# MoE weights read in 8 KB and 4 KB runs, with a gather that reads h at a step of four floats

## The chip, the cores and the metric

The kernel runs on one core of one Trainium2 chip. The metric is the device time in microseconds, the median of the runs shown.

## What is computed

The program is two blocks of a model on 256 tokens of 1024 features, float32. The part that matters is the mixture of experts that ends each of the two layers of the second block: a router picks one of 4 groups and 2 of its 4 experts for each token, and each of the 16 experts is a gated network of width 512,

`y = (silu(x @ w_gate[e]) * (x @ w_up[e])) @ w_down[e]`

with w_gate and w_up of 1024 x 512 and w_down of 512 x 1024. All weights of all experts are read: 16 x 3 x 2 MB = 96 MB in each layer, 192 MB in all.

## The kernel before, in words

`MoeQueue` (lines 56 to 117) is the stream of weights for a memory attention and the MoE layer behind it. Its constructor lists the chunks in the order of use: for every pair of experts p = 0 to 7, four chunks of w_gate, four of w_up and four of w_down, each of 1 MB. `fetch` (78) issues one load for each free slot, on SP's queue (line 85); `done` (113) gives the slots of used chunks back and fetches again. Slots are tiles of 8 KB on each of 128 partitions; some slots come in two halves, and their chunk is then loaded as two pieces. A chunk of w_gate or w_up holds 512 of the 1024 input features; partition p of it holds rows p, 128 + p, 256 + p and 384 + p of the 512, four runs of 2 KB in memory. A chunk of w_down holds all 512 inner features and 512 of the 1024 output columns, again four runs of 2 KB on each partition.

`moe` (1571) makes eight passes q = 0 to 7, one for each pair of experts, with the two experts side by side in the 128 output partitions (64 slots for tokens each). The steps of a pass, by line:

- L1639: gate, then up. The gathered tokens `xg` are the stationary operand, the weights the moving one. For a gate or up: 8 features of 128 x 2 experts = 16 matmuls of 128 x 64 by 512 columns. A float32 matmul has two records in the trace, so a pass has 64 records.
- L1644, L1645: silu on ACT and the product on DVE give `hid`.
- L1625 (`scatter`): the pass before's result Y is added to the tokens' sums, 8 matmuls, in float32r.
- L1612, L1614 (`select_T`): the selection is transposed (sT), and the tokens' weights (cs) are fetched.
- L1654, L1656: `hid` is transposed to `hT`.
- L1604 (`gather`, for pass q + 1): token selection by matmul. A block of 128 tokens by 128 features of h is the stationary operand, the 0/1 selection `sel` the moving one (128 columns); 8 feature blocks x 2 token blocks = 16 matmuls, 32 records. ACT and DVE copy the result to `xg` (L1606). There are 8 gathers in each layer: one ahead of pass 0, and one in each of passes 0 to 6.
- L1668: down, 16 matmuls into two accumulators `pd[0]`, `pd[1]` of 512 columns each, 32 records: first all of half hf = 0, then hf = 1.
- L1674, L1675: ACT and DVE split each half of pd into two float32r parts, Y.

In pass 7 the code scatters half 0 before the second half of down is evicted, and a branch for overfull experts (`moe_dense`, L1665 to L1667) stands in the middle of down.

The order of the instructions on each engine is settled when the program is built: the framework takes the code's order as a priority and may put an instruction with ready inputs ahead of one that it thinks must wait. TensorE then runs its list in that fixed order.

The lines that the change touches:

Of the kernel before, what the change touches and what calls it, by code (L numbers as in the profile page):

```python
# [11 lines left out]
F32 = mybir.dt.float32  # L12
# [41 lines left out]


class MoeQueue:
    """Weight chunks of a memory attention and a MoE layer in the order of use: slots of a ring, and some filled only once."""

    def __init__(self, nc, wq, wo, wg, wu, wd):
        self.nc, self.ring, self.free, self.loaded, self.used = nc, [], [], [], 0  # L60
        self.queue = []
        if wq is not None:
            self.queue += [(wq[:, c * 256:c * 256 + 256].rearrange("(k p) f -> p k f", p=128), 8) for c in range(4)]
            self.queue += [(wo[k * 128:k * 128 + 256].rearrange("(a p) f -> p a f", p=128), 2) for k in range(0, 8, 2)]
        for p in range(8):
            for w in (wg, wu, wd):
                for c in range(2):
                    for e in (2 * p, 2 * p + 1):
                        cut = w[e, :, c * 512:c * 512 + 512] if w is wd else w[e, c * 512:c * 512 + 512, :]
                        self.queue.append((cut.rearrange("(k p) f -> p k f", p=128), 4))  # L70

    def add(self, pool, n):
        self.free += [(pool, "mw", True, 1)] * n
# [4 lines left out]
    def fetch(self, n=99):  # L78
        while n and self.free and len(self.loaded) < len(self.queue):
            ap, a = self.queue[len(self.loaded)]  # L80
            slot = self.free.pop(0)
            v, m = [], a // slot[3]
            for u in range(slot[3]):
                t = slot[0].tile([128, 2048 // slot[3]], F32, tag=slot[1], name="mw").rearrange("p (k f) -> p k f", k=m)
                self.nc.sync.dma_start(t, ap[:, u * m:u * m + m])
                v.append(t)
            self.loaded.append(v[0] if slot[3] == 1 else v)
            self.ring.append(slot)
            n -= 1
# [30 lines left out]
class Block:  # L120
# [1450 lines left out]
    def moe(self, h, x32, r, li, last=False):  # L1571
        nc, i, tc = self.nc, self.i, self.tc
        vec, act, pe = nc.vector, nc.scalar, nc.tensor
        tt, mm = vec.tensor_tensor, pe.matmul
        mq, self.moe_queue, self.pending = self.moe_queue, None, None
        C, pos, iota = r["C"], r["pos"], r["iota"]
        with ExitStack() as es:
            mo = es.enter_context(tc.tile_pool(name="mo", bufs=1))
            mb = es.enter_context(tc.tile_pool(name="mb", bufs=self.extra))
            if last:  # L1580
                mq.once(self.mp, "mk")
                mq.once(self.mp, "mv")
            mq.add(mb, self.extra)
            mq.once(self.xp, "xl")
            mq.once(self.gp, "nrm", 2)
            mq.once(self.gp, "g", 2)
            mq.once(self.xp, "xh")
            mq.fetch()

            def select(q):  # L1590
                sel = mo.tile([128, 2, 128], F32, name="sel", bufs=2)
                for t in range(2):
                    tt(sel[:, t].rearrange("p (e s) -> p e s", e=2), iota.unsqueeze(1).broadcast_to([128, 2, 64]),
                       pos[:, t, 2 * q:2 * q + 2].unsqueeze(2).broadcast_to([128, 2, 64]), op=ALU.is_equal)
                return sel

            def gather(sel):
                xg = mo.tile([128, 8, 128], F32, name="xg")
                for g in range(2):
                    p = self.ps()  # L1600
                    for u in range(4):
                        f = 4 * g + u
                        for t in range(2):
                            mm(p[:, u * 128:u * 128 + 128], h[:, t, f * 128:f * 128 + 128], sel[:, t],  # L1604
                               start=t == 0, stop=t == 1)
                    (act.copy, vec.tensor_copy)[g](xg[:, 4 * g:4 * g + 4], p.rearrange("p (u s) -> p u s", u=4))  # L1606
                return xg

            def select_T(q, sel):
                p = self.ps()  # L1610
                for t in range(2):
                    pe.transpose(p[:, t * 128:t * 128 + 128], sel[:, t], self.ident)  # L1612
                for t in range(2):
                    mm(p[:, 256:258], sel[:, t], C[:, t, 2 * q:2 * q + 2], start=t == 0, stop=t == 1)  # L1614
                sT = mo.tile([128, 256], F32R, name="sT")
                cs = mo.tile([128, 1], F32, name="cs")
                act.copy(sT, p[:, 0:256])
                for e in range(2):
                    vec.tensor_copy(cs[64 * e:64 * e + 64], p[64 * e:64 * e + 64, 256 + e:257 + e])
                return sT, cs  # L1620

            def scatter(q, hf, sT, Y):
                for t in range(2):
                    for n in range(2):
                        mm(acc[t][hf], sT[:, t * 128:t * 128 + 128], Y[hf][n], start=q == 0 and n == 0, stop=q == 7 and n == 1)  # L1625

            acc = self.accs()
            stats = [self.small(8, "ln") for _ in range(2)]
            sel = select(0)
            xg = gather(sel)  # L1630
            prev = None
            for q in range(8):
                gu = []
                for m in range(2):
                    w = mq.take(4)
                    ps = self.ps()
                    for k in range(8):
                        for e in range(2):
                            mm(ps[64 * e:64 * e + 64], xg[:, k, e * 64:e * 64 + 64], mq.slab(w[2 * (k // 4) + e], k % 4),  # L1639
                               start=k == 0, stop=k == 7)  # L1640
                    mq.done(4)
                    gu.append(ps)
                hid = mo.tile([128, 512], F32, name="hid")
                act.activation(hid, gu[0], AF.Silu)  # L1644
                tt(hid, hid, gu[1], op=ALU.mult)  # L1645
                if q == 0:
                    over = nc.values_load(r["cnti"][0:1, 0:1], min_val=0, max_val=512)
                if prev is not None:
                    for hf in range(2):
                        scatter(q - 1, hf, *prev)  # L1650
                sT, cs = select_T(q, sel)
                p = self.ps()
                for f in range(4):
                    pe.transpose(p[:, f * 128:f * 128 + 128], hid[:, f * 128:f * 128 + 128], self.ident)  # L1654
                hT = mo.tile([128, 4, 128], F32, tag="hT", name="hT")
                vec.tensor_copy(hT, p.rearrange("p (f s) -> p f s", f=4))  # L1656
                if q < 7:
                    sel = select(q + 1)
                    xg = gather(sel)
                w = mq.take(4)  # L1660
                pd = [self.ps(), self.ps()]
                for hf in range(2):
                    for k in range(4):
                        if q == 7 and hf * 4 + k == 6:
                            with tc.If(over > 64):  # L1665
                                self.moe_dense(mo, h, li, r["Co"])
                        for e in range(2):  # L1667
                            mm(pd[hf][64 * e:64 * e + 64], hT[:, k, 64 * e:64 * e + 64], mq.slab(w[2 * hf + e], k),  # L1668
                               start=k == 0, stop=k == 3)
                mq.done(4)  # L1670
                Y = []
                for hf in range(2):
                    y = [mo.tile([128, 512], F32R, tag="hT" if hf and n else "Y%d%d" % (hf, n), name="Y") for n in range(2)]
                    act.activation(y[0], pd[hf], AF.Copy, scale=cs)  # L1674
                    vec.scalar_tensor_tensor(y[1], pd[hf], cs, y[0], op0=ALU.mult, op1=ALU.subtract)  # L1675
                    Y.append(y)
                    if q == 7 and hf == 0:
                        scatter(7, 0, sT, Y)
                        self.deep_add(h, acc, stats, 0)
                prev = sT, Y  # L1680
            scatter(7, 1, *prev)
            self.deep_add(h, acc, stats, 1)
        x = None if last else self.xT()
        self.layer_norm_both(h, acc, stats, li, 2, *(x or ()))
        return x
# [323 lines left out]
```

## Time and profile before

| | |
|---|---|
| median of 3 runs | 1748.44 us (1744.04 to 1748.51) |
| span of the profiled execution, first to last instruction | 1741.2 us |
| TensorE busy | 1619.0 us, 93% of the span |
| mean granted TensorE clock | 0.958 |
| bytes moved by DMA | 375.39 MB in 230353 packets |

The span is that of one profiled execution. Only its span is given; the three timed runs are 2.8 to 7.3 us above it, which is what lies around the first and last instruction. The two MoE stages are about 1062 to 1296 us and 1497 to 1730 us after the start.

### The profile page before, as it was taken

To read this page: it belongs to the slowest core of one execution; us is meant where nothing else is said; L and a number is where in the kernel's file an instruction comes from. 1 tells how busy PE (TensorE), PEld (TensorE's weight loads), DVE (VectorE), ACT (ScalarE), POOL (GpSimd) and SP (SyncE) were. 2 spreads that over 40 slices of the span, in tenths; PEclk is the share of its full clock that TensorE was granted. 3 is DMA by queue.
4 is the path that set the end of the run, shared out by engine and by line. 5 is a ranking of instruction groups with operands and counts; after the bars stand their busy time and mean duration, and the time that the engine had idled before them with its cause. 6 is when DMAs were issued, how large, how long until landed. Compare 5 with 4: busy or idle time off the path is not lost. (4 is left out here: it accounts for less than half of the span.)

```text
span 1741.2 us, 26063 instructions
## 1 busy us (share of the span) xinstructions
PE 1619.0 (93%) x10383; PEld 1213.0 (70%) x10383; DVE 888.9 (51%) x1864; ACT 699.2 (40%) x1288; POOL 186.8 (11%) x153
## 2 busy tenths in 40 slices
PE   7899999879899999999999899999979989999995
PEld 6778999758788778999887785444427778544532
DVE  3567655498857567665568643111126964311112
ACT  5676455345434546554467432010116643201101
POOL 4610000056623110000101000000000000000000
PEclk9999999989969998999999899999989999999998
DMA  9324653432321329643661948999948177899983
GB/s 346 134 97 148 216 187 129 125 106 85 97 69 58 108 81 308 206 159 121 226 233 49 339 173 330 387 387 387 386 146 284 74 254 258 325 387 386 387 321 127
DMA packets 230353, 375.39 MB, mean 216 GB/s; under 512 B 17092, under 2 KB 105932, under 8 KB 230220
## 3 DMA queue, kind: packets, MB, share of 16 engines
q1 hardware_dynamic: 215616, 359.88, 58.7%
q10 hardware_dynamic: 14604, 13.71, 2.6%
q8 instruction: 86, 1.41, 0.3%
q14 instruction: 47, 0.39, 0.1%
HBM read 372.52 MB, written 1.05 MB: 215 GB/s over the span
## 5 line engine op out<-in xcount | busy, mean ns | idle before, releaser
L191 ACT CAST wh<-w 128x1024 fp32r<-128x1024 f32 (+1 forms) x253 | 260.3, 1039 | 232.5 <-PE mm L216 123.1
L192 DVE TENSOR_TENSOR wl<-w,wh 128x1024 fp32r<-128x1024 f32 (+1 forms) x214 | 257.1, 1210 | 151.9 <-ACT wh L191 151.4
L1639 PE MATMUL mm<-mw,xg 128*64 128x512 f32 x1024 | 230.2, 594 | 0.0
L217 PE MATMUL mm<-xh,wl 128*128 128x256 f32 x800 | 227.1, 284 | 0.0
L216 PE MATMUL mm<-xl,wh 128*128 128x256 f32 x800 | 226.9, 284 | 0.0
L215 PE MATMUL mm<-xh,wh 128*128 128x256 f32 x800 | 226.6, 283 | 0.0
L1639 PEld LDWEIGHTS mm<-mw,xg 128*64 128x64 f32 x1024 | 73.7, 137 | 144.0 <-issue 142.5
L215 PEld LDWEIGHTS mm<-xh,wh 128*128 128x128 f32 x800 | 151.9, 190 | 1.9
L216 PEld LDWEIGHTS mm<-xl,wh 128*128 128x128 f32 x800 | 151.3, 189 | 2.3 <-DVE xl L252 0.3
L217 PEld LDWEIGHTS mm<-xh,wl 128*128 128x128 f32 x800 | 151.5, 189 | 0.0
L1668 PE MATMUL mm<-mw,hT 128*64 128x512 f32 x512 | 118.7, 596 | 1.7 <-issue 1.7
L215 PE MATMUL acc<-wh,xh 128*128 128x512 f32 x284 | 112.9, 403 | 1.6 <-ACT xh L249 0.9
L216 PE MATMUL acc<-wl,xh 128*128 128x512 f32 x284 | 114.0, 402 | 0.0
L217 PE MATMUL acc<-wh,xl 128*128 128x512 f32 x284 | 113.3, 401 | 0.0
L192 POOL TENSOR_TENSOR wl<-w,wh 128x1024 fp32r<-128x1024 f32 x39 | 93.4, 2404 | 79.4 <-ACT wh L191 73.9
L1645 DVE TENSOR_TENSOR hid<-hid,mm 128x512 f32<-128x512 f32 x16 | 11.0, 687 | 168.3 <-PE mm L1639 168.3
L1668 PEld LDWEIGHTS mm<-mw,hT 128*64 128x64 f32 x512 | 36.6, 137 | 69.2 <-issue 67.5
L1675 DVE SCALAR_TENSOR_TENSOR Y<-mm,cs,Y 128x512 fp32r<-128x512 f32 x32 | 24.0, 751 | 114.2 <-ACT Y L1674 114.2
L1674 ACT ACTIVATE Y<-mm,cs 128x512 fp32r<-128x512 f32 x32 | 22.0, 687 | 146.8 <-PE mm L1668 146.8
L215 PE MATMUL acc<-wh,fh 128*128 128x512 f32 x176 | 69.5, 395 | 0.0
L217 PE MATMUL acc<-wh,fl 128*128 128x512 f32 x176 | 69.5, 396 | 0.0
L216 PE MATMUL acc<-wl,fh 128*128 128x512 f32 x176 | 69.3, 394 | 0.0
(529 smaller groups left out, 3127.8 us busy)
## 6 DMA issues: line engine op xcount, KB each, us to landing
mw<-in_moe_w_gate_dram SPq DMA_DIRECT2D x61, 1024.0 KB, 14.2
mw<-in_moe_w_up_dram SPq DMA_DIRECT2D x60, 1024.0 KB, 14.3
mw<-in_moe_w_down_dram SPq DMA_DIRECT2D x57, 1024.0 KB, 14.1
w<-in_ffn_w_gate_dram SPq DMA_DIRECT2D x22, 1024.0 KB, 5.9
w<-in_ffn_w_up_dram SPq DMA_DIRECT2D x22, 1024.0 KB, 6.7
w<-in_ffn_w_down_dram SPq DMA_DIRECT2D x22, 1024.0 KB, 6.3
w<-in_attn_w_qkv_dram SPq DMA_DIRECT2D x12, 1024.0 KB, 10.8
w<-in_a_w_in_dram SPq DMA_DIRECT2D x12, 1024.0 KB, 10.6
```

What stands on the lines that cost most here:

```text
L191: nc.scalar.copy(r[0], raw)
L192: (lo_eng or nc.vector).tensor_tensor(r[1], raw, r[0], op=ALU.subtract)
L215: mm(out, lhs[0], rhs[0], start=start, stop=False)
L216: mm(out, lhs[0], rhs[1], start=False, stop=False)
L217: mm(out, lhs[1], rhs[0], start=False, stop=stop)
L1639: mm(ps[64 * e:64 * e + 64], xg[:, k, e * 64:e * 64 + 64], mq.slab(w[2 * (k // 4) + e], k % 4), start=k == 0, stop=k == 7)
L1645: tt(hid, hid, gu[1], op=ALU.mult)
L1668: mm(pd[hf][64 * e:64 * e + 64], hT[:, k, 64 * e:64 * e + 64], mq.slab(w[2 * hf + e], k), start=k == 0, stop=k == 3)
L1674: act.activation(y[0], pd[hf], AF.Copy, scale=cs)
L1675: vec.scalar_tensor_tensor(y[1], pd[hf], cs, y[0], op0=ALU.mult, op1=ALU.subtract)
```

## The change

Three things change. The chunks of w_gate and w_up are cut so that partition p holds rows 4p to 4p + 3 of the 512, one run of 8 KB (two of 4 KB where the slot comes in halves). So that the input features fit, the gather takes as its stationary operand features 4q + u of a half instead of 128 adjacent ones: 128 elements of h at a step of four floats, 16 bytes. And for passes 0 to 6 the chunks of w_down hold 256 inner features and all 1024 output columns, two runs of 4 KB, with the loop of L1668 turned round: the inner feature block outside, the output half inside. Pass 7 keeps its w_down chunks and loop order. Numbers and sizes of loads and of matmuls stay.

```diff
@@ MoeQueue.__init__
         for p in range(8):
-            for w in (wg, wu, wd):
+            for w in (wg, wu):
                 for c in range(2):
                     for e in (2 * p, 2 * p + 1):
-                        cut = w[e, :, c * 512:c * 512 + 512] if w is wd else w[e, c * 512:c * 512 + 512, :]
-                        self.queue.append((cut.rearrange("(k p) f -> p k f", p=128), 4))
+                        self.queue.append((w[e, c * 512:c * 512 + 512, :].rearrange("(p k) f -> p (k f)", k=4), 4))
+            for c in range(2):
+                for e in (2 * p, 2 * p + 1):
+                    if p == 7:
+                        self.queue.append((wd[e, :, c * 512:c * 512 + 512].rearrange("(k p) f -> p k f", p=128), 4))
+                    else:
+                        self.queue.append((wd[e, c * 256:c * 256 + 256, :].rearrange("(k p) f -> p k f", p=128), 2))
@@ MoeQueue.fetch
-            v, m = [], a // slot[3]
+            v, m, n1 = [], a // slot[3], 2048 // slot[3]
             for u in range(slot[3]):
-                t = slot[0].tile([128, 2048 // slot[3]], F32, tag=slot[1], name="mw").rearrange("p (k f) -> p k f", k=m)
-                self.nc.sync.dma_start(t, ap[:, u * m:u * m + m])
-                v.append(t)
+                t = slot[0].tile([128, n1], F32, tag=slot[1], name="mw")
+                if len(ap.shape) == 2:
+                    self.nc.sync.dma_start(t, ap[:, u * n1:u * n1 + n1])
+                    v.append(t.rearrange("p (k f) -> p k f", k=m))
+                else:
+                    t = t.rearrange("p (k f) -> p k f", k=m)
+                    self.nc.sync.dma_start(t, ap[:, u * m:u * m + m])
+                    v.append(t)
@@ moe, gather
+            hk = h.rearrange("p t (c q k) -> p t c k q", c=2, k=4)
...
-                            mm(p[:, u * 128:u * 128 + 128], h[:, t, f * 128:f * 128 + 128], sel[:, t],
-                               start=t == 0, stop=t == 1)
+                            mm(p[:, u * 128:u * 128 + 128], hk[:, t, g, u], sel[:, t], start=t == 0, stop=t == 1)
@@ moe, down
-                for hf in range(2):
-                    for k in range(4):
-                        if q == 7 and hf * 4 + k == 6:
-                            with tc.If(over > 64):
-                                self.moe_dense(mo, h, li, r["Co"])
-                        for e in range(2):
-                            mm(pd[hf][64 * e:64 * e + 64], hT[:, k, 64 * e:64 * e + 64], mq.slab(w[2 * hf + e], k),
-                               start=k == 0, stop=k == 3)
+                order = [(hf, k) for hf in range(2) for k in range(4)] if q == 7 else [(hf, k) for k in range(4) for hf in range(2)]
+                for n, (hf, k) in enumerate(order):
+                    if q == 7 and n == 6:
+                        with tc.If(over > 64):
+                            self.moe_dense(mo, h, li, r["Co"])
+                    for e in range(2):
+                        if q == 7:
+                            b = mq.slab(w[2 * hf + e], k)
+                        else:
+                            b = mq.slab(w[2 * (k // 2) + e], k % 2)[:, hf * 512:hf * 512 + 512]
+                        mm(pd[hf][64 * e:64 * e + 64], hT[:, k, 64 * e:64 * e + 64], b, start=k == 0, stop=k == 3)
```

## Rows read from the trace of the kernel before

**Rows 1.** The page: span, busy time, and GB/s in 40 slices.

```profile
span 1741.2 us, 26063 instructions
PE 1619.0 (93%) x10383; PEld 1213.0 (70%) x10383; DVE 888.9 (51%) x1864; ACT 699.2 (40%) x1288; POOL 186.8 (11%) x153
GB/s 346 134 97 148 216 187 129 125 106 85 97 69 58 108 81 308 206 159 121 226 233 49 339 173 330 387 387 387 386 146 284 74 254 258 325 387 386 387 321 127
```

**Rows 2.** Windows of layer 0's MoE: busy by engine, PEclk, DMA share, GB/s.

```profile
1080.00:1197.00 117.00, 117.00 (x625) 55.00 (x626) 18.82 (x38) 12.48 (x22) 0.00 (x0) 1.00 1.05 387
1272.00:1284.00 12.00, 10.39 (x47) 3.67 (x44) 1.38 (x2) 0.11 (x1) 0.08 (x1) 1.00 0.02 7
```

**Rows 3.** Waits of the weight-load side, 1060 to 1280 us: total, times, longest.

```profile
PEld mm L1639 <- DMA mw<-in_moe_w_down_dram: 0.7, 2, 0.4
```

**Rows 4.** Timeline of PE, layer 0, pass 3 and the start of 4.

```profile
1142.92 13.90 PE L1639 MATMUL mm<-mw,xg 128*64 128x512 f32 x64
...
1159.79 3.74 PE L1604 MATMUL mm<-sel,h 128*128 128x128 f32 x32
1163.45 7.09 PE L1668 MATMUL mm<-mw,hT 128*64 128x512 f32 x32
1170.37 13.90 PE L1639 MATMUL mm<-mw,xg 128*64 128x512 f32 x64
```

**Rows 5.** Timeline of PE, layer 0, passes 5 and 6.

```profile
1197.80 7.89 PE L1639 MATMUL mm<-mw,xg 128*64 128x512 f32 x34
...
1229.68 1.07 PE L1639 MATMUL mm<-mw,xg 128*64 128x512 f32 x2
...
1247.41 0.66 PE L1654 MATMUL mm<-c_ident,hid 128*128 128x128 f32 x4 [0.78 <-DVE hid L1645]
...
1251.57 4.50 PE L1668 MATMUL mm<-mw,hT 128*64 128x512 f32 x18
1256.06 0.74 PE L1625 MATMUL acc<-Y,sT 128*128 128x512 f32 x2
1256.72 3.65 PE L1668 MATMUL mm<-mw,hT 128*64 128x512 f32 x14
1260.30 0.73 PE L1625 MATMUL acc<-Y,sT 128*128 128x512 f32 x2
1260.96 1.07 PE L1639 MATMUL mm<-mw,xg 128*64 128x512 f32 x2
```

**Rows 6.** Timeline of PE, layer 1, starts of passes 6 and 7.

```profile
1660.74 1.02 PE L1639 MATMUL mm<-mw,xg 128*64 128x512 f32 x2
...
1694.45 1.07 PE L1639 MATMUL mm<-mw,xg 128*64 128x512 f32 x2
```

**Rows 7.** The page: all packets; and a window while 4 KB runs of attn_w_qkv load.

```profile
DMA packets 230353, 375.39 MB, mean 216 GB/s; under 512 B 17092, under 2 KB 105932, under 8 KB 230220
10.00:16.00 6.00, 5.77 (x26) 4.40 (x25) 5.37 (x8) 5.10 (x8) 0.55 (x1) 1.00 1.04 397
```

**Rows 8.** Groups by shape, PEld: busy, mean ns of one.

```profile
L1639 PEld LDWEIGHTS mm<-mw,xg 128*64 128x64 f32 x1024 | 73.7, 137 | 144.0 <-issue 142.5 <-DMA mw<-in_moe_w_down_dram 0.7 <-SPq L1665 0.3
...
L1614 PEld LDWEIGHTS mm<-C,sel 128*128 128x128 f32 x64 | 8.4, 191 | 0.0
```

**Rows 9.** Timeline of PEld, pass 3 of layer 0.

```profile
1158.85 0.53 PEld L1614 LDWEIGHTS mm<-C,sel 128*128 128x128 f32 x4
```

**Rows 10.** Groups by shape, DVE: L829 reads at a 64 B step, the others contiguously.

```profile
L829 DVE TENSOR_TENSOR tmp<-aT 128x225 f32<-128x225 f32 x2 | 1.1, 546 | 0.0
L829 DVE TENSOR_TENSOR tmp<-aT 128x100 f32<-128x100 f32 x2 | 0.6, 313 | 0.0
L1885 DVE TENSOR_TENSOR s<-acc,sc 128x384 f32<-128x384 f32 x8 | 4.4, 552 | 0.2
L544 DVE TENSOR_TENSOR ft<-gt,mm 128x256 f32<-128x256 f32 x44 | 18.3, 416 | 7.4 <-PE mm L217 5.0 <-ACT gt L542 2.4
```

**Rows 11.** The page: eviction of Y on ACT.

```profile
L1674 ACT ACTIVATE Y<-mm,cs 128x512 fp32r<-128x512 f32 x32 | 22.0, 687 | 146.8 <-PE mm L1668 146.8
```

## The prediction

> **What bounds the kernel now.** I read the page first: TensorE is busy 93% of the span, and the DMA slices show where the MoE weights pass: four slices in a row at 386 or 387 GB/s in layer 0, and the like in layer 1 [rows 1]. So two candidates for the bound of these stages, and the stage's own views must say which. The windows of layer 0's MoE show both full: in 117 us TensorE has no idle time, its granted clock is 1.00 (the higher level, 2.4 GHz), and the transfer engines have a share of 1.05 at 387 GB/s [rows 2]. The waits decide: in 220 us the largest wait of the gate and up matmuls for loads is 0.7 us, in two places together [rows 3]. TensorE sets the pace; the loads had a head start and just keep it. They are done early too: after 1272 us the window holds 7 GB/s [rows 2], and TensorE has been in the last pass since 1260.96 [rows 5].
>
> The timeline then gives the price list of a pass: pass 3 of layer 0 takes 1170.37 - 1142.92 = 27.45 us, its gather 1163.45 - 1159.79 = 3.66 us, its down 1170.37 - 1163.45 = 6.92 us, all without a gap [rows 4]. Passes 5 and 6 are longer with the same matmuls: their scatters stand inside down and between the first gate matmuls, and `hid` is waited for [rows 5]. That is an order fixed at the build, not a wait for data.
>
> **The transfers.** 64 chunks of gate and up in a layer go from 512 runs each to 128, and 28 of the 32 down chunks from 512 to 256: 64 x 384 + 28 x 256 = 31,744 packets fewer in a layer, 63 thousand in both, of 230 thousand [rows 7]. What a longer run does to the rate: 2 KB runs have 387 GB/s [rows 2], a window in which 4 KB runs make most of the bytes has 397 [rows 7], 2.6% more; no row has 8 KB. The 96 MB of a layer (100.7 MB in the profile's units, 260 us at 387) would be through 7 us sooner. I cost this at nothing: TensorE's work hides it, and a faster stream could return little more in this stage than those 0.7 us; if the rate fell by the same 2.6%, the end 7 us later would still come with TensorE busy in the last pass. Ends: -1 to +1 us. SP issues as many loads as before, so nothing moves in its queue.
>
> **The gather.** This is the term that decides. Each layer has 8 gathers of 32 records, 16 x 32 = 512 records in all, every one on TensorE's path. A record now costs 3.66 / 32 = 114 ns [rows 4]. What sets this? A load of 128 columns has a duration of 191 ns, one of 64 columns 137 [rows 8], so 54 / 64 = 0.84 ns a column and 108 ns for 128. Where the matmul behind the load has only two columns, four loads take 0.53 us, so they follow each other by (0.53 - 0.19) / 3 = 113 ns [rows 8, 9]. So loads at full pace take 113 of the 114 ns: there is a slack of 1 ns, and whatever the step of 16 bytes adds to a load shows at once. It can't shorten a record, as the load was contiguous and its matmul stays. The lower end is 0.
>
> No row shows TensorE reading at a step. The nearest is VectorE at L829, which reads one operand at a step of 64 bytes: from 100 to 225 elements it goes from 313 to 546 ns, 1.86 ns an element, against (552 - 416) / 128 = 1.06 in contiguous operations [rows 10]. A step costs VectorE 0.80 ns an element, a factor of 1.75. Carried to the load in three ways: by the factor, 108 x 0.75 - 1 = 80 ns a record, 41 us; by the added time, 128 x 0.80 - 1 = 101 ns, 52 us; by 1.86 ns an element outright, 128 x 1.86 + 5 - 114 = 129 ns, 66 us. Between 0 and 66 I take the added time, 52 us: the memory is the same one, and L829 is the only row of a stepped read that I can put a slope to. A gather would take 6.9 us, and the pass 30.7.
>
> **Down.** Loop order and cut: same 32 records, same four chunks taken at once. `pd[0]` is now complete two records before the end instead of at half time. In passes 0 to 4 its eviction (ACT 0.69 us [rows 11], DVE after it) has the 13.9 us of the next gate and up [rows 4] before scatter needs Y, so it costs nothing. Where a scatter stood inside down (three places: passes 5 and 6 of layer 0, pass 6 of layer 1) it can't stand there any more. Such a down took 1260.30 - 1251.57 less 0.66 for the two scatter matmuls, 8.07 us against 6.92 [rows 4, 5]: 1.15 us three times, 3.5 us back at best. If the scatter then stands right behind down, it waits for the eviction, 0.69 us three times, 2.1 us. I take -1; ends -3.5 and +2.
>
> **Sum.** 52 - 1 = +51 us. The profile's span would go from 1741.2 to 1792; the median lies 7.2 us above that span, so 1748.4 + 51 = 1799. Own range of this case: from 41 - 4.5 to 66 + 3, that is 1785 to 1817.
>
> **Rival 1: the step is free, and the order stays.** TensorE may have enough reads under way that a load takes 108 ns at any step. For it: a load's 0.84 ns a column is already twice the 0.42 ns in which the array takes a moving column at 2.4 GHz, so something else than the memory may set it. Against: L829. Then only down and the transfers remain: 1747, between 1744 and 1751, which a measurement can't tell from no change (0.3% is 5.2 us). The Trainium skill, "SBUF — State Buffer", section "Door 1: The DMA port swizzle (why `[64,N]` ≈ `[32,N]`)", says that consecutive reads must hit a 16-byte line twice for full bandwidth, and then that "how far you can stride for free depends on dtype: 4 fp32"; the step here is exactly four floats. By that last sentence the time would be the 1747 of this rival; by the first one the load pays; no run so far shows which.
>
> **Rival 2: faster, because the order of passes 5 to 7 is settled anew.** The build put scatters early in passes 5 and 6. Were the new program ordered like pass 3 throughout, layer 0 would get back: from the start of pass 5 to that of pass 7 63.16 us [rows 5], less two passes of 27.45 and 1.3 us for four scatter matmuls of pass 6 already done, 7.0 us. In layer 1 pass 6 takes 1694.45 - 1660.74 = 33.71 [rows 6], less 27.45 and 1.3, 5.0 us. Together 12 us: 1736, if the step is free. It decides for faster from about half of that on. For it: loads in longer runs may count as earlier at the build, and the scatter's old place inside down is closed. Against: in both layers the loads would still be the slower of the two (12.6 MB a pass at 387 GB/s is 32.5 us against 27.45), so that the build has the same reason to put other work first. With the step's cost it gives 1787, inside the range of the first case.
>
> **Rival 3: the transfers gain more than I think**, 8 KB runs being well above 397 GB/s. It changes nothing while TensorE sets the pace, so it is hidden anyway, and ends at 1747 too.
>
> **How the numbers follow.** The stepped load costs something over 0.3% with a chance of 0.50; free with about the same order 0.26 (rivals 1 and 3); free with a better order 0.24. The predicted time is that of the first, 1799. The cases lie on both sides: the range reaches from 1737, which leaves out the better half of rival 2, to 1815, which leaves out the dearest loads. Faster 0.24, same 0.26, slower 0.50.
>
> **What would show it.** In the profile after: PEld at the gather's line, records 200 ns or more apart and a gather near 6.9 us in the timeline (3.66 if rival 1 holds); pass 3 at 30.7 us; packets near 167 thousand; GB/s in the MoE slices between 387 and 397, or less where TensorE takes the weights more slowly; waits of L1639 for loads still under 2 us in a layer; passes 5 and 6 with down in one piece, and 27 to 28 us (less the gather's surplus) if rival 2 is right. I am wrong if the gather keeps 3.7 us, or if TensorE turns out to wait for loads.

## The result, and the profile after

| | before | after |
|---|---|---|
| median, measured side by side, 4 runs each | 1748.47 us (1744.04 to 1752.74) | 1804.86 us (1800.51 to 1807.12) |
| ratio after / before | | 1.0331, 95% interval 1.0304 to 1.0358 |
| span of the profiled execution | 1741.2 us | 1805.3 us |

The change makes the kernel 3.3% slower, 56 us. Each time lies about 1.8 us above the span of its own execution (1807.12 and 1805.3 for the profiled one after, the slowest of its four). So the 2.8 to 7.3 us between the times before and the one span given there, and the 7.2 us that the prediction names, are for the most part differences between executions, and not what lies around the first and last instruction.

The page of the kernel after, its lines for the span, TensorE (PE) and its weight loads (PEld), VectorE (DVE) and ScalarE (ACT), the transfer rate in 40 slices and the packets:

```profile
span 1805.3 us, 26048 instructions
PE 1682.7 (93%) x10383; PEld 1279.4 (71%) x10383; DVE 886.3 (49%) x1864; ACT 699.3 (39%) x1288; POOL 186.9 (10%) x153
GB/s 345 136 77 178 188 195 94 173 49 114 98 48 83 85 198 226 205 184 98 302 70 252 219 244 392 396 408 378 114 125 253 44 351 269 331 408 393 171 329 92
DMA packets 167761, 375.39 MB, mean 208 GB/s; under 512 B 17092, under 2 KB 105932, under 8 KB 152140
```

PE has 63.7 us more busy time and PEld 66.4 more, for the same number of instructions [rows 1]. The packets fell by 62,592. So the loads got the longer runs that were wanted, and TensorE got slower. Where, the groups by shape tell (busy time, mean ns of one; idle before). First the gather's weight load in the kernel before, then load and matmul in the kernel after:

```profile
L1604 PEld LDWEIGHTS mm<-sel,h 128*128 128x128 f32 x512 | 60.2, 196 | 0.7 <-PE mm L1522 0.7
```

```profile
L1617 PE MATMUL mm<-sel,h 128*128 128x128 f32 x512 | 122.7, 400 | 0.6 <-DVE lg L1543 0.6
L1617 PEld LDWEIGHTS mm<-sel,h 128*128 128x128 f32 x512 | 120.8, 329 | 0.7 <-PE mm L1532 0.7
```

A load of 128 columns takes 133 ns longer, 1.04 ns a column. The timeline of PE in pass 3 of layer 0 (start, length, engine, line, count), after:

```profile
1132.71 13.90 PE L1651 MATMUL mm<-mw,xg 128*64 128x512 f32 x64
...
1149.55 7.63 PE L1617 MATMUL mm<-sel,h 128*128 128x128 f32 x32
1157.10 7.09 PE L1684 MATMUL mm<-mw,hT 128*64 128x512 f32 x32
1164.02 13.90 PE L1651 MATMUL mm<-mw,xg 128*64 128x512 f32 x64
```

Gate and up last 13.90 us and down 1164.02 - 1157.10 = 6.92 us, both as before [rows 4]. The gather alone has grown, from 3.66 to 1157.10 - 1149.55 = 7.55 us, that is from 114 to 236 ns a record, and the pass from 27.45 to 31.31 us. 512 records by 122 ns are 62.5 us.

From the first gather to the last scatter, layer 0's MoE grew from 1295.40 - 1055.59 = 239.8 to 1331.40 - 1061.63 = 269.8 us and layer 1's from 1728.46 - 1489.46 = 239.0 to 1792.63 - 1525.17 = 267.5: 58.5 us together. The other 5.6 us of the difference of the two spans lie outside the two MoE stages, where nothing was changed; the medians, 56.4 us apart, don't have them.

The windows of layer 0's MoE after (us, busy time of PE, PEld, DVE, ACT, POOL, then PEclk, DMA share, GB/s), and the one row of waits of the gate and up loads for a transfer, 1060 to 1335 us:

```profile
1090.00:1220.00 130.00, 130.00 (x606) 71.95 (x607) 17.55 (x37) 12.30 (x21) 0.00 (x0) 1.00 0.99 398
1226.00:1300.00 74.00, 72.33 (x317) 36.57 (x314) 9.73 (x18) 7.23 (x12) 0.00 (x0) 1.00 0.63 250
```

```profile
PEld mm L1651 <- DMA mw<-in_moe_w_down_dram: 0.6, 2, 0.3
```

TensorE is busy without a gap in the first of these windows and for 72.33 of 74 us in the second, at a granted clock of 1.00 (the higher level), and waits 0.6 us in all for weights, against 0.7 before [rows 3] and 0.3 more on a load of w_gate. It hardly waits less, since there was nothing to wait less for. Passes 5 and 6 keep their early scatter, but down stands now in one piece, with the scatter behind it:

```profile
1226.65 7.89 PE L1651 MATMUL mm<-mw,xg 128*64 128x512 f32 x34
...
1252.99 7.14 PE L1684 MATMUL mm<-mw,hT 128*64 128x512 f32 x32
1260.10 1.52 PE L1637 MATMUL acc<-Y,sT 128*128 128x512 f32 x4
1261.55 1.07 PE L1651 MATMUL mm<-mw,xg 128*64 128x512 f32 x2
...
1295.87 1.07 PE L1651 MATMUL mm<-mw,xg 128*64 128x512 f32 x2
```

### The profile page after: what moved, and what is told of

Its sections match the earlier page's. It is cut to its first block, busy times and chain, and to the rows that moved or that the text cites. A ratio compares the mean times of both kernels' runs of the same rounds, so it can differ in the third digit from the quotient of the medians.

```text
span 1805.3 us, 26048 instructions
## 1 busy us (share of the span) xinstructions
PE 1682.7 (93%) x10383; PEld 1279.4 (71%) x10383; DVE 886.3 (49%) x1864; ACT 699.3 (39%) x1288; POOL 186.9 (10%) x153
## 3 DMA queue, kind: packets, MB, share of 16 engines
q1 hardware_dynamic: 153024, 359.88, 54.5%
q8 instruction: 86, 1.41, 0.3%
## 5 line engine op out<-in xcount | busy, mean ns | idle before, releaser
L1617 PE MATMUL mm<-sel,h 128*128 128x128 f32 x512 | 122.7, 400 | 0.6 <-DVE lg L1543 0.6
L1617 PEld LDWEIGHTS mm<-sel,h 128*128 128x128 f32 x512 | 120.8, 329 | 0.7 <-PE mm L1532 0.7
```

Source lines behind the costliest of these rows:

```text
L1617: mm(p[:, u * 128:u * 128 + 128], hk[:, t, g, u], sel[:, t], start=t == 0, stop=t == 1)
```

## The experiments

The theory: the whole loss is the stepped weight load, and longer runs give nothing because TensorE sets the pace. Rivals: something else of the change costs (the loop of down, the transfers, the order), or the step costs less than it seems and an order covers part of it.

### Take the parts apart

**adjacent**: the kernel after, gathering adjacent columns of h again.

```diff
-mm(p[:, u * 128:u * 128 + 128], hk[:, t, g, u], sel[:, t], ...)
+mm(p[:, u * 128:u * 128 + 128], h[:, t, f * 128:f * 128 + 128], sel[:, t], ...)
```

> The changed kernel with the gather reading 128 adjacent features again, and nothing else undone, so that it multiplies the wrong features by the weights and its output is not the reference's. Theory S (the stepped weight load is the whole loss): a gather is back from 7.56 to 3.67 us, 16 gathers give back 62 us, and the time is 1740 to 1748. Rival T (the longer runs or the down loop cost something too): some of the loss stays, 1755 or more; if they were the whole of it, 1800 to 1805.

Measured: 1747.24 us (1741.16 to 1751.91), ratio to before 1.0012 (0.9998 to 1.0026). The loss is gone, and no gain is to be seen, although the transfers run faster than in any kernel with 2 KB runs. The page's rates:

```profile
GB/s 346 132 98 146 218 175 140 112 118 74 108 67 56 109 76 313 199 163 122 219 239 48 339 172 330 414 416 416 351 86 287 73 277 233 325 415 417 335 311 124
```

416 instead of 387 GB/s in the MoE's full slices [rows 1], 7.5% more, is worth nothing that can be measured here.

**step4**: the kernel before, with the step of the gather alone.

```diff
+hk = h.rearrange("p t (c q k) -> p t c k q", c=2, k=4)
-mm(p[:, u * 128:u * 128 + 128], h[:, t, f * 128:f * 128 + 128], sel[:, t], ...)
+mm(p[:, u * 128:u * 128 + 128], hk[:, t, f // 4, f % 4], sel[:, t], ...)
```

> The kernel before with only the gather's step of four floats, weights and loops as they were, so that the features don't fit the weights and the output is not the reference's. Theory S: 512 records at 236 instead of 114 ns, +62 us, 1806 to 1813, slightly above the changed kernel, which has the down loop's gain of up to 3.5 us. Rival T: 1748 to 1760.

Measured: 1804.76 us (1802.01 to 1806.31), ratio 1.0346 (1.033 to 1.0362), and to the nanosecond the loads of the kernel after:

```profile
L1606 PEld LDWEIGHTS mm<-sel,h 128*128 128x128 f32 x512 | 120.8, 329 | 0.7 <-PE mm L1522 0.7
```

One edit in one operand, with the old transfers, the old down and the old order, makes the whole loss.

**down_only**: the kernel before, with the change's cut of w_down and its loop.

```diff
-            for w in (wg, wu, wd):
+            for w in (wg, wu):
...
+                        self.queue.append((wd[e, c * 256:c * 256 + 256, :].rearrange("(k p) f -> p k f", p=128), 2))
...
-                for hf in range(2):
-                    for k in range(4):
+                order = [(hf, k) for hf in range(2) for k in range(4)] if q == 7 else [(hf, k) for k in range(4) for hf in range(2)]
```

> The kernel before with only the w_down part: 4 KB runs and the turned loop in passes 0 to 6; gate, up and gather as before. Theory S: within 4 us of the kernel before, 1744 to 1750, since the transfers are hidden and a down that scatters no longer cut is worth at most 1.2 us in three places. Rival T: clearly slower, by over 5 us.

Measured: 1744.49 us (1741.52 to 1747.97) against 1744.44 before, ratio 0.9997 (0.9984 to 1.001). Neither the order of the loop nor 4 KB runs (389 to 397 GB/s in the full slices of its page) move the time.

### What the step costs, by its size

**step2** and **step8**: as step4, with `k=2` and `k=8` in the rearrangement, so that neighbours in the load are 8 or 32 bytes apart.

> The kernel before with the gather at a step of two floats (8 bytes), weights as they were, so that the output is not the reference's. If the price is paid for each new 16 bytes that a load touches (1.88 ns each, hidden as far as the load has four or two elements from it), two elements share one: 128 x 0.94 + 5 = 125 ns a record, +6 us, 1751 to 1757. If it is paid for each element that isn't adjacent to the one before: as with four floats, 1806 to 1813. If a step of two is free: 1744 to 1750.

> The kernel before, with only the gather's stationary operand read at a step of 8 floats (32 bytes); the features of h reach the gate and up matmuls in another order than that of their weights, so the output is another. If the price is that of opening a 16-byte stretch for every element, a step of 4 floats has reached its end: PEld mean 329 ns, gather 7.5 us a pass, time 1800 to 1810 us. If the price grows with the distance (as it grew from a step of 2, +6 ns a record, to a step of 4, +122 ns), it goes on: PEld over 450 ns, gather over 11 us, time over 1860 us.

Measured: step2 1749.96 us (1749.53 to 1751.76), ratio 1.0034 (1.0021 to 1.0047); step8 1806.32 us in one run, so without an interval. The loads, of step2 and then of step8:

```profile
L1606 PEld LDWEIGHTS mm<-sel,h 128*128 128x128 f32 x512 | 66.6, 209 | 0.7 <-PE mm L1522 0.7
```

```profile
L1606 PEld LDWEIGHTS mm<-sel,h 128*128 128x128 f32 x512 | 123.3, 334 | 0.7 <-PE mm L1522 0.7
```

With gather and down of step2's timeline, then of step8's:

```profile
1138.11 3.93 PE L1606 MATMUL mm<-sel,h 128*128 128x128 f32 x32
1141.97 7.09 PE L1669 MATMUL mm<-mw,hT 128*64 128x512 f32 x32
```

```profile
1144.06 7.77 PE L1606 MATMUL mm<-sel,h 128*128 128x128 f32 x32
1151.77 7.09 PE L1669 MATMUL mm<-mw,hT 128*64 128x512 f32 x32
```

A gather at a step of two floats takes 1141.97 - 1138.11 = 3.86 us, 121 ns a record, 6 or 7 more than adjacent columns. At four floats a record costs 122 more than adjacent columns, and eight floats add little to that: (1151.77 - 1144.06) / 32 = 241 ns against 236. So from 16 to 32 bytes the price doesn't grow with the distance. It is there at both steps, where no two neighbours lie within the same 16 bytes, and all but gone at 8 bytes, where two do. No step between 8 and 16 bytes was run.

**moving4**: the kernel before, with the weights of gate and up, the moving operand, read at a step of four floats.

```diff
-mm(ps[...], xg[...], mq.slab(w[2 * (k // 4) + e], k % 4), ...)
+mm(ps[...], xg[...], mq.slab(w[2 * (k // 4) + e], k % 4).rearrange("p (n s) -> p s n", s=4), ...)
```

> The kernel before, with the moving operand of the gate and up matmuls (the weights, 512 columns) read at a step of 4 floats and the gather as it was; the output's columns come in another order. It asks whether the price belongs to the stationary load alone. If every read of the array at a 16-byte step pays as the weight load does (1.04 ns a column more), a record of 512 columns lasts some 530 ns longer, and 256 pairs of records give 136 us if a pair runs side by side, 272 us if not: 1880 to 2020 us. If the moving side streams a step of 16 bytes at its own pace, the matmul stays at 594 ns and the time at 1742 to 1750 us.

Measured: 1988.61 us in one run, 243.7 us more than the 1744.95 before. Its group, and gate and up of one pass in its timeline:

```profile
L1639 PE MATMUL mm<-mw,xg 128*64 128x512 f32 x1024 | 476.7, 1079 | 0.0
```

```profile
1144.65 28.97 PE L1639 MATMUL mm<-mw,xg 128*64 128x512 f32 x64
```

Gate and up of a pass take 28.97 instead of 13.90 us [rows 4]; 16 passes by 15.07 us are 241 us, nearly the whole difference. 32 pairs of records share the 15.07 us: 471 ns for 512 columns, 0.92 ns a column. The moving side pays as the stationary one does. (The expectation counted 256 pairs of records where the two layers have 512, each pair running side by side, so its lower figure belongs with the doubled count, at 272 us; 244 were measured.)

### Can the runs be had without the price?

**copy**: the kernel after, but h is copied once a layer into the order of the runs, and the gather loads adjacent columns of the copy. The copy takes the memory of one spare slot of the weight queue.

```diff
-hk = h.rearrange("p t (c q k) -> p t c k q", c=2, k=4)
+hv = h.rearrange("p t (c q k) -> p t c k q", c=2, k=4)
+hc = mo.tile([128, 2, 1024], F32, name="hc")
+hk = hc.rearrange("p t (c k q) -> p t c k q", c=2, k=4)
+for t in range(2):
+    for c in range(2):
+        (act.copy, vec.tensor_copy)[c](hk[:, t, c], hv[:, t, c])
-b.extra = 2
+b.extra = 1
```

> The changed kernel with the 8 KB runs and the cut of w_down kept, but the strided read moved out of TensorE: once a layer four copies of 128x512 (two on ScalarE, two on VectorE) write h in the order of the runs, and all 512 gather records load adjacent columns of that copy. If the loss is the price of the stepped weight load, paid 512 times and here only in four copies of about 1.1 us, it is gone: PEld 196 to 203 ns, gather 3.7 us, and 1744 + (0 to 2 x 2.2) = 1744 to 1752 us. If something else of the change costs (the one slot of memory fewer for the queue of weights, the order of features, the loop of the down projection), a part of the 56 us stays: over 1760 us.

Measured: 1749.76 us (1748.27 to 1751.72), ratio 1.0023 (1.0008 to 1.0037). The full slices of its page run at 414 to 418 GB/s, and some 52 of the 56 us are back. The copies themselves, from the view of that tile (count, then least, median and greatest ns, first and last start):

```profile
L1612 ACT COPY hc<-h x4: 1138/1142/1150, 1046.1 to 1489.2; 128x512 f32<-128x512 f32 x4
L1612 DVE COPY hc<-h x4: 611/630/642, 1046.7 to 1489.9; 128x512 f32<-128x512 f32 x4
```

So the change can be had almost for nothing, and is worth nothing: the step was paid 512 times by TensorE, and is paid here by two engines that have time. What TensorE sees of the copies is a later start of the router's matmuls in each layer, the row of layer 0 before and then with the copies:

```profile
1047.51 1.92 PE L1519 MATMUL mm<-x,wr 128*20 128x128 f32 x16 [0.29 <-ACT x L258]
```

```profile
1047.79 1.92 PE L1529 MATMUL mm<-x,wr 128*20 128x128 f32 x16 [0.88 <-ACT x L268]
```

That is 0.59 us more, and the same in layer 1, 1.2 of the 4 us. The rest can't be put down to the copies: in this profile the 28 last records of the two first gathers take 5.79 and 5.55 us at granted clocks of 0.54 and 0.57, against 3.32 and 4.95 us at 1.00 and 0.65 before; but in the profile of `order` below, which has no copy, they take 6.02 and 5.63 us at 0.52 and 0.56.

### The order of passes 5 to 7

**order**: the kernel before, with the scatter held back until the last up matmul is issued.

```diff
-mm(ps[64 * e:64 * e + 64], xg[...], ...)
+up = mm(ps[64 * e:64 * e + 64], xg[...], ...)
 ...
-for hf in range(2):
-    scatter(q - 1, hf, *prev)
+with tc.issue_after(up.ins):
+    for hf in range(2):
+        scatter(q - 1, hf, *prev)
```

> The kernel before, with one edit: the scatter of the pass before is held back until the last up matmul is issued, in all passes, so that passes 5 and 6 of both layers run in the order of pass 3. Rival 2's premise, that the early scatter costs 3 us in each of these four passes, gives 1744 - 12 = 1733 us (1731 to 1738) and pass lengths of 27.5 us throughout. If the early scatter only moves a wait (PE waits then for the evictions elsewhere in the same pass), the time stays 1742 to 1748 us, and passes 5 and 6 still last about 30 us though the scatter stands in its place.

Measured: 1737.06 us (1732.77 to 1740.09), ratio 0.9948 (0.9929 to 0.9966), faster by 8 us in the medians and 9 by the ratio. The timeline of PE in pass 6 of layer 0:

```profile
1232.05 7.89 PE L1639 MATMUL mm<-mw,xg 128*64 128x512 f32 x34
1239.87 0.44 PE L1612 MATMUL mm<-c_ident,sel 128*128 128x128 f32 x2
...
1240.58 7.08 PE L1639 MATMUL mm<-mw,xg 128*64 128x512 f32 x30
1247.59 2.14 PE L1625 MATMUL acc<-Y,sT 128*128 128x512 f32 x8
1249.57 0.60 PE L1655 MATMUL mm<-c_ident,hid 128*128 128x128 f32 x4
...
1253.67 7.09 PE L1669 MATMUL mm<-mw,hT 128*64 128x512 f32 x32
1260.59 7.89 PE L1639 MATMUL mm<-mw,xg 128*64 128x512 f32 x34
```

The scatter has its place, `hid` isn't waited for, and a pass takes 1260.59 - 1232.05 = 28.54 us instead of 31.28 [rows 5]. It isn't the 27.45 of pass 3: the transposes of the selection still cut gate and up in two, and 7.89 + 7.08 is 1.07 us more than the 13.90 of the uncut piece. From the gather of pass 0 (the one for pass 1) to the last scatter, layer 0 goes from 217.9 to 212.3 us and layer 1 from 215.5 to 211.9: 9.2 us, in line with the times.

**order_again**, **down_order** (with the w_down of down_only) and **copy_order** (the copy kernel with the scatter held back), measured together:

> The kernel with the scatter held back in every pass, once more, as the measure for the two runs beside it: 0.995 of the kernel before (0.993 to 0.997), 1733 to 1740 us.

> The scatter held back, and w_down loaded in runs of 4 KB with its loop as in the change; gate and up and the gather as before. If transfers stay hidden, the two edits add up to the gain of the order alone, since the w_down part gave nothing by itself: 1733 to 1740 us, within 3 us of the run with the order alone. If the order has brought PE up to the transfers (its profile has one wait of PE on a w_up load, 0.9 us), the faster loads of w_down show now: 1 to 3 us under it.

> The changed kernel with the copy of h (long runs everywhere, gather from adjacent columns) and the scatter held back. Additive: +4 for the copies and -8 for the order make 1740 us (1736 to 1745), over the run with the order alone. If the transfers bind once the order is mended, the rate of 8 KB runs takes back the copies' price: 1736 us or under, no slower than the order alone.

| | median (range), us | ratio to before (1744.14 us) |
|---|---|---|
| order_again | 1734.94 (1729.86 to 1738.74) | 0.9941 (0.9922 to 0.996) |
| down_order | 1733.39 (1731.73 to 1735.3) | 0.994 (0.9923 to 0.9958) |
| copy_order | 1735.54 (1734.06 to 1737.8) | 0.9952 (0.9934 to 0.9969) |

All three beat both kernels, and their intervals overlap: the order makes the gain, and the longer runs add nothing to it that can be told. The copies' 4 us aren't seen again in copy_order. That the long runs take them back there, as its second hypothesis has it, finds no support in the profiles: TensorE's loads wait for weights for 0.6 us in the two MoE stages of order_again together and for 0.9 in those of copy_order, so there are no 4 us of waiting to win back. The copies may cost less than the first comparison said, but the intervals are as wide as the difference, and this stays open.

## Why the prediction was right, and where its sizes were off

**What bounds the stage: right.** TensorE, with transfers that just keep up. `adjacent` shows it: rates up by 7.5%, time within 0.3%.

**The gather: right in its mechanism, too small by a sixth.** The prediction saw that a load at full pace leaves 1 ns of slack in a record, so that whatever the step adds shows at once; `step4` and the timeline after confirm it. The term that was mis-sized is the price of the step: I took VectorE's added time, 0.80 ns an element, 101 ns a record and 52 us. Measured are 122 ns a record. TensorE's load adds 1.04 ns a column to its 0.84, 1.88 together, which is close to VectorE's 1.86 ns an element outright [rows 10]; this third way, 129 ns and 66 us, was the nearest of the three. Whether that is more than a coincidence isn't shown: VectorE's own copy at a step of 16 bytes, in `copy`, takes 630 ns for 512 elements, 1.23 each at most. The added time rested on weak ground, too. Its 1.06 ns for contiguous elements is the slope between two different operations, and the stepped row belongs to another engine at another step. That 1799 came within 6 us of the median has some luck in it: it was the middle one of three figures, and that there is a price at all had a chance of 0.50.

In the MoE stages the terms add up so: 14 gathers inside the passes by 7.55 - 3.66 = 3.89 us are 54.5; the first gathers of the two layers add 3.4 and 2.4 us, from the start of a gather to that of the gate behind it (6.54 to 9.96 us and 8.17 to 10.53). Together that is 60.2. With -1.7 for down (below) it makes the 58.5 us found. Against the forecast of 52 the gather has 60.2 - 52 = 8.2 us more, and the median came out 5.9 above 1799.

The first gathers pay less than the others, and their rows show why. Their last 28 records and the gate behind them, layers 0 and 1, before and then after:

```profile
1058.81 3.39 PE L1604 MATMUL mm<-sel,h 128*128 128x128 f32 x28
1062.13 13.95 PE L1639 MATMUL mm<-mw,xg 128*64 128x512 f32 x64
...
1492.68 5.02 PE L1604 MATMUL mm<-sel,h 128*128 128x128 f32 x28
1497.63 13.95 PE L1639 MATMUL mm<-mw,xg 128*64 128x512 f32 x64
```

```profile
1064.86 6.80 PE L1617 MATMUL mm<-sel,h 128*128 128x128 f32 x28
1071.59 13.95 PE L1651 MATMUL mm<-mw,xg 128*64 128x512 f32 x64
...
1529.01 6.76 PE L1617 MATMUL mm<-sel,h 128*128 128x128 f32 x28
1535.70 13.95 PE L1651 MATMUL mm<-mw,xg 128*64 128x512 f32 x64
```

In layer 0 the surplus of the first four records disappears in a wait for VectorE ahead of these rows (1.41 us before, 0.92 after). In layer 1 the clock comes in, too. Before the change its mean over these records was 1.00 in layer 0 and 0.65 in layer 1, where 1.00 is the level of 2.4 GHz and the lower level is 1.2; in the stretch ahead of them TensorE had been busy for 1.52 of 3.20 us and for 1.42 of 3.10. The adjacent gather takes 119 and 177 ns a record there. After the change the clock was 0.74 and 0.62, and the stepped gather takes 240 and 239 ns, hardly more than the 236 at 1.00. So the stepped gather barely gets slower with the clock, while the adjacent one does, and the price of the step is smaller where the clock is low.

**Down: right.** From the start of pass 5 to that of pass 7, layer 0 took 63.16 us before [rows 5] and 1295.87 - 1226.65 = 69.22 after; less two gathers' surplus of 3.89 that is 1.72 us won. Pass 6 of layer 1 won 1.21 in the same way (33.71 us before [rows 6], 1758.46 - 1722.07 = 36.39 after, less 3.89). A down with the scatter behind it takes 1260.10 - 1252.99 = 7.11 us against 6.92, so the wait for the eviction is 0.2 us and not the 0.7 taken for the end of +2; `pd[0]` is complete four records before the end of down, and not two. Pass 7, where the scatter stands between more of the gate matmuls in layer 0, gave back 1.25 in the two layers, which the forecast didn't have. -1.7 us in all, where -1 was taken with ends of -3.5 and +2; `down_only` has -0.5 (-2.8 to +1.7).

**Transfers: right about their worth, too low on the rate.** The packets fell by 62,592, where 63,488 were counted. The 397 GB/s of 4 KB runs was carried over to 8 KB; `adjacent` shows 416. Rival 3 was therefore true as a fact and without effect, as it said.

**Rival 1, the step is free: refuted** by `step4` and by the profile after. The Trainium skill, "SBUF — State Buffer", section "Door 1: The DMA port swizzle (why `[64,N]` ≈ `[32,N]`)", has the two sentences that the prediction set against each other. The runs agree with the first: with two hits in a 16-byte line the price is small (step2: 6 ns a record), with one it is not (step4: 122, step8: 127). Its "4 fp32", taken as a step that is free, does not hold here: the free step is less than that. That it is the shared line which counts, and not a distance of more than 8 bytes, no run here can tell.

**Rival 2, the order settled anew: it wasn't**, as the prediction held more likely; what made the build keep the order no run shows. Its price was near: 12 us were counted for an order like pass 3's, and `order` gains 8 to 9, since gate and up stay cut in two. That the kernel before leaves this gain on the table was seen in the rows, but the change doesn't touch it.

## What to carry to other kernels

Before a load is made faster, look at what waits for it: here some 1 us of waiting was all that did, and 7.5% more transfer rate bought nothing. Before a layout is paid for with a stepped read, see which engine reads it and how often: a step of 16 bytes, at which no two neighbours share 16, doubled the gather's record (114 to 236 ns) and the gate and up stream alike (13.90 to 28.97 us), while one copy a layer on two engines with time to spare does the same rearrangement for 4 us or less. And where passes of equal work have unequal lengths in the timeline, the order of the build is worth a look.

## What the hardware showed that I had not expected

- The price of a step is a threshold and not a slope: 114 ns a record for adjacent columns, 121 at 8 bytes, 236 at 16, 241 at 32. It sets in between 8 and 16 bytes.
- A stepped gather takes 240 and 239 ns a record at granted clocks of 0.74 and 0.62, and 236 at 1.00; an adjacent one goes from 114 to 119 at 1.00 to 177 at 0.65.
- The price falls on the moving operand too: 0.92 ns a column, 241 us in `moving4` (one run).
- The engines differ: ScalarE's copy at a step of 16 bytes takes 1142 ns for 512 elements, where its copy of `xg`, adjacent but out of PSUM, takes 585; VectorE's takes 630, less than the 692 of its own copy of `xg`, although VectorE's stepped operation at L829 has a slope of 1.86 ns an element [rows 10]. What makes VectorE's copy cheap was not tried.
- The rate of one stream of loads by the length of its runs, in full slices or windows of the MoE: 387 GB/s at 2 KB, 389 to 397 where w_down has 4 KB, 416 at 8 KB (gate and up) with 4 KB (down).
